# Weights in contiguous tiles, and both halves of the weight split on GpSimd, in a one-core hybrid layer

## The chip, the cores and the metric

The kernel runs on one core of one Trainium2 chip. A core has TensorE (PE, matrix products into PSUM), VectorE (DVE), ScalarE (ACT), GpSimd (POOL) and SyncE (SP, which here issues the DMAs), and 16 DMA engines between HBM and the on-chip buffer. The metric is the device time of one launch in microseconds (us), the median of three runs; lower is better.

## The reference

One layer of a diffusion backbone for 256 context tokens and 2048 latent tokens of width 1024, all in float32:

```python
mod_ctx = (jnp.einsum('d,dn->n', jax.nn.silu(c_ctx), w_ada[l]) + b_ada[l])[None]
mod_lat = jnp.einsum('bd,dn->bn', jax.nn.silu(c), w_ada[l]) + b_ada[l]
...
shift, scale, gate = jnp.split(mod, 3, axis=-1)
h = rmsnorm(x, g_pre) * (1.0 + scale[:, None]) + shift[:, None]
proj = jnp.einsum('btd,dn->btn', h, w_in)
...                       # NA, DeltaNet and pooling branches on slices of proj
merged = (g_dn * jnp.einsum('btw,wd->btd', y_dn, w_br_dn)
          + g_na * jnp.einsum('btw,wd->btd', y_na, w_br_na)
          + g_pl * jnp.einsum('btw,wd->btd', y_pl, w_br_pl))
out = rmsnorm(jnp.einsum('btd,de->bte', merged, w_out), g_post)
return x + gate[:, None] * out, k_na, v_na, s_fin
```

`w_in` has 8208 columns: q, k, v of the DeltaNet branch (1536), its gate path z (512), 16 columns for beta and a, q, k, v and z of the neighbourhood attention (4 x 512), u and z of the pooling branch (2 x 512), and the three merge gates (3072). The DeltaNet branch runs a short convolution with a SiLU over its q, k, v and then a recurrence over chunks; the attention branch has windows of 8 x 16 on a grid of 32 x 64 and all context keys.

## The kernel before

**Tiles.** The tokens are five blocks: C (256 context tokens) and L0 to L3 (512 latent tokens each). h is kept transposed, eight tiles of 128 channels by the block's tokens. Products of float32 are made of three products of a reduced type: each operand is split into a high part (a cast to fp32r) and a low part (the remainder), and `mm3` adds high x high, high x low and low x high. `split` (L167 to 170) is the helper for this: a cast on ACT (L169), then a subtraction on an engine that the caller names (L170).

**Weights of the input projection.** A unit is 128 columns of `w_in`. `load_w` (L552) loads it in two DMAs of 256 KB, each four 128x128 tiles side by side, into `wraw` (three buffers). ACT casts the 128x512 into `whi`, GpSimd subtracts into `wlo`; both have five buffers (`WBUFS`), two for a unit. `proj` (L566) then runs 24 matrix products for a block into a PSUM buffer `mm` (two of these). In HBM a row of such a tile is four pieces of 512 B, 32,832 B apart.

**Stages.** At the start `ada_part` (L427) loads eight pieces of `w_ada` of 1 MB each for shift and scale (a row is eight pieces of 1 KB) and multiplies them by the two conditioning vectors; beside it x of C and L0 is normalised and transposed, and `make_h` (L506) makes h: ACT the high part `hL0h`, DVE the full value `hf` (also kept in buffers named `x`, L522), GpSimd or DVE the low part `hL0l` (L523). Then `qkv` (L613) goes over C, L0 and L1, and again over L2 and L3. For each unit of q, k, v of DeltaNet, ACT copies the PSUM to `xcL` (L630) or `xcC` (L589), and `conv_silu` (L572) does DVE, then a tanh on ACT (`cv_th`, L580), then DVE, and stores to `d_dn`. Then, for eight units of attention q and k, ACT copies to `nqk` (L656, L658). Between these the 32 pieces of the attention's value weights (128x256, 128 KB) are loaded into the same three `nqk` buffers and split into `wvh` and `wvl` (L642 to L647), and the values are computed. Then `rest` (L1106) runs over the other units of `w_in`, for C, L2 and L3 and then for L0 and L1: gate paths (`zc`, copied at L1123), merge gates (a tanh `th`, L1131) and pooling. The branches (DeltaNet, whose steps end in names like `v` L1041; attention, with `pr`, `oT`, `klo`) run beside the projections. `final` (L1473) loads `w_br` in 120 tiles of 256 KB (`br_r`, four pieces of 512 B a row), splits them and merges.

**Order.** PE runs in the order of the program text. There a planner decides: `mm` advances a clock `self.t` by an estimate, `use` (L96) books time on `v`, `s` or `g` (DVE, ACT, GpSimd), and `poll` (L71) takes up the side branches whenever their due time has come. ACT, DVE, GpSimd and SP are ordered by the framework's scheduler, except where `dma_here` or `keep_in_program_order` fixes an instruction. All DMAs are issued from SP.

Of the kernel before, what the change touches and what calls it, by code (L numbers as in the profile page):

```python
# [7 lines left out]
F32 = mybir.dt.float32  # L8
# [3 lines left out]
ALU = mybir.AluOpType  # L12
# [4 lines left out]
P = 128  # L17
D = 1024
KT = 8
# [6 lines left out]
C_QKV, C_DZ, C_BA = 0, 1536, 2048  # L26
C_NQ, C_NK, C_NV, C_NZ = 2064, 2576, 3088, 3600
# [11 lines left out]
NQ = 3  # L39
# [8 lines left out]
class Net:  # L48
# [378 lines left out]
    def ada_part(self, q):  # L427

        nc = self.nc
        ps = self.mmp.tile([P, 512], F32, name="mm")  # L430
        for s in range(2):
            t = self.ap.tile([P, KT, 256], F32, name="w_ada", bufs=3)
            self.dma_here(t, self.a["w_ada"].rearrange("(k p) n -> p k n", p=P)[:, :, s * D + q * 256:s * D + q * 256 + 256])
            for k in range(KT):
                for c in range(2):
                    self.mm(ps[64 * s + 32 * c:64 * s + 32 * c + 32, :P], self.ada_sc[:, k, :], t[:, k, c * P:(c + 1) * P], k == 0, k == KT - 1)
        r = self.wp.tile([P, 4, P], F32, name="wraw", bufs=3)[:, 0]
        nc.scalar.copy(r, ps[:, :P])
        tp = self.ax1()[:, :P]
        self.tr(tp, r, self.ident)  # L440
        part = lambda t: t.rearrange("p (s k) x -> p s k x", s=2)[:, :, 2 * q:2 * q + 2]
        nc.vector.tensor_tensor(part(self.mod), tp.rearrange("p (s k x) -> p s k x", s=2, k=2)[:, :, :, 0:2],
                                part(self.cc["b_ada"].rearrange("p (c o) -> p c o", o=1)).broadcast_to([P, 2, 2, 2]), ALU.add)
        k = slice(2 * q, 2 * q + 2)
        g = self.cc["g_pre"]
        nc.vector.scalar_tensor_tensor(self.A[:, k], self.mod[:, 8 + 2 * q:10 + 2 * q, :], 1.0,
                                       g[:, k].rearrange("p (k o) -> p k o", o=1).broadcast_to([P, 2, 2]), ALU.add, ALU.mult)

    def ada_gate(self):

        nc, a = self.nc, self.a
        ps = self.ax1()

        for k in range(KT):
            t = self.ap.tile([P, D], F32, name="w_ada", bufs=3)
            self.dma_here(t, a["w_ada"][k * P:(k + 1) * P, 2 * D:])
            yield self.t + 5
            for c in range(4):
                self.mm(ps[32 * c:32 * c + 32, :256], self.ada_sc[:, k, :], t[:, c * 256:(c + 1) * 256], k == 0, k == KT - 1)
        r, bg, gp = (self.ap.tile([P, 256], F32, name=f"ada_{x}", bufs=1) for x in "rbg")  # L460
        for c in range(4):
            q = slice(32 * c, 32 * c + 2)
            for t, v in ((bg, a["b_gate"]), (gp, a["g_post"])):
                self.dma(t[q], bass.AP(v.tensor, v.offset + c * 256, [[0, 2], [1, 256]]))
            nc.vector.tensor_tensor(r[q], ps[q, :256], bg[q], ALU.add)
            nc.vector.tensor_tensor(r[q], r[q], gp[q], ALU.mult)
            self.dma(self.d_gg[:, c * 256:(c + 1) * 256], r[q])
# [84 lines left out]
    def load_w(self, c0, dma=None):  # L552
        hi, lo = [], []
        for k in (0, 4):
            raw = self.wp.tile([P, 4, P], F32, name="wraw", bufs=3)
            (dma or self.dma)(raw, self.a["w_in"].rearrange("(k p) n -> p k n", p=P)[:, k:k + 4, c0:c0 + P])
            h = self.wp.tile([P, 4, P], F32R, name="whi", bufs=WBUFS)
            l = self.wp.tile([P, 4, P], F32R, name="wlo", bufs=WBUFS)
            self.split(raw, h, l, self.nc.gpsimd)
            self.use("s", 0.52)  # L560
            self.use("g", 1.23)
            hi += [h[:, i] for i in range(4)]
            lo += [l[:, i] for i in range(4)]
        return hi, lo
# [48 lines left out]
    def qkv(self, h, second, nxt, first=None):  # L613
        nc = self.nc
# [21 lines left out]
        wv = [[self.qp.tile([P, KT, 264], F32R, name=x, bufs=2) for x in ("wvh", "wvl")] for _ in range(2)]  # L636

        raw = self.qp.tile([P, KT, 16], F32, name="wba", bufs=1)
        self.dma(raw, self.a["w_in"].rearrange("(k p) n -> p k n", p=P)[:, :, C_BA:C_BA + 16])
        for c in range(2):  # L640
            self.split(raw[:, :, 8 * c:8 * c + 8], wv[c][0][:, :, 256:264], wv[c][1][:, :, 256:264], nc.vector)
        for ct in range(8):  # L642
            for k in (2 * ct % 8, 2 * ct % 8 + 1):
                c = ct // 4
                raw = self.qp.tile([P, 512], F32, name="nqk", bufs=NQ)
                self.dma(raw[:, :256], self.a["w_in"][k * P:(k + 1) * P, C_NV + c * 256:C_NV + c * 256 + 256])
                self.split(raw[:, :256], wv[c][0][:, k, :256], wv[c][1][:, k, :256], nc.gpsimd)  # L647
            isq = ct < 4
            w = self.load_w(C_NQ + ct * P)
            r = slice((ct % 4) * P, (ct % 4 + 1) * P)  # L650
            for b in h:
                n = BLK[b]
                ps = self.proj(w, h[b], n)
                e = self.qp.tile([P, 512], F32, name="nqk", bufs=NQ)
                if isq:
                    nc.scalar.activation(e[:, :n], ps[:, :n], AF.Copy, scale=0.125)  # L656
                else:
                    nc.scalar.copy(e[:, :n], ps[:, :n])  # L658
                if b == "C":
                    self.dma((self.d_nq if isq else self.d_nk)["C"][r, :], e[:, :n])  # L660
                    if not isq:
                        self.add(self.new_k(e, r))
                else:
                    o = int(b[1]) * 512 + (0 if isq else CTX)
                    self.dma((self.d_nq if isq else self.d_nk)["L"][r, o:o + 512], e)

        for b in sorted(h, key=lambda b: b == "C"):
            for j in range(0, BLK[b] // P, 2):
                for c in range(2):
                    e = self.qp.tile([P, 528], F32, name="ev", bufs=2)  # L670
                    t = (0 if b == "C" else 2 + 4 * int(b[1])) + j
                    for i in range(2):
                        ps = self.mmp.tile([P, 512], F32, name="mm")
                        s = slice((j + i) * P, (j + i + 1) * P)
# [798 lines left out]
    def final(self, b, ys, nxt):  # L1473
        nc, f = self.nc, self.fin
        v, s = nc.vector, nc.scalar
        n = BLK[b]
# [6 lines left out]
        for m in range(KT):  # L1483
            if m:
                next(self.wo, None)
            acc = None
            for bi in range(3):
                raw = f.tile([P, 4, P], F32, name="br_r", bufs=BR)
                self.dma(raw, self.a["w_br"][bi].rearrange("(k p) n -> p k n", p=P)[:, :, m * P:(m + 1) * P])
                wh = f.tile([P, 4, P], F32R, name="br_h", bufs=BH)  # L1490
                wl = f.tile([P, 4, P], F32R, name="br_l", bufs=BH)
                self.split(raw, wh, wl, v if b == "C" and bi else nc.gpsimd)
                gt = f.tile([P, 512], F32, name="gt", bufs=GT)
                self.dma(gt[:, :n], self.d_g[b][m, :, bi, :])
                ps = self.mmp.tile([P, 512], F32, name="mm")
                yh, yl = ys[bi]
                for k in range(4):
                    self.mm3(ps[:, :n], wh[:, k, :], wl[:, k, :], yh[:, k, :n], yl[:, k, :n], k == 0, k == 3)
                v.scalar_tensor_tensor(gt[:, :n], gt[:, :n], 1.0, ps[:, :n], ALU.add, ALU.mult)  # L1499
                if acc is None:  # L1500
                    acc = gt
                else:
                    v.tensor_tensor(acc[:, :n], acc[:, :n], gt[:, :n], ALU.add)  # L1503
            mh[m] = self.fw.tile([P, 512], F32R, name="mh", bufs=8)
            ml[m] = self.fw.tile([P, 512], F32R, name="ml", bufs=8)
            s.activation(mh[m][:, :n], acc[:, :n], AF.Copy, scale=0.25)
            v.scalar_tensor_tensor(ml[m][:, :n], acc[:, :n], 0.25, mh[m][:, :n].bitcast(F32), ALU.mult, ALU.subtract)
# [40 lines left out]
def lay_out(i):  # L1548

    import numpy as np  # L1550
    f = lambda x: np.ascontiguousarray(np.asarray(x))
    cols = lambda x, k: f(np.asarray(x).reshape(k, P).T)
    d = {}
# [4 lines left out]
    d["cache_k"] = f(i["cache_k_na"]).reshape(CTX, 512)  # L1558
    d["cache_v"] = f(i["cache_v_na"]).reshape(CTX, 512)
    d["state_dn"] = f(i["state_dn"]).reshape(2, 4, P, P)  # L1560
    d["w_ada"] = f(i["w_ada"]).reshape(D, 3 * D)
    ba = np.asarray(i["b_ada"]).reshape(3 * D)
    d["b_ada"] = cols(ba[:2 * D], 16)
    d["b_gate"] = f(ba[2 * D:])
    d["g_pre"] = cols(i["g_pre"], KT)
    d["g_post"] = f(i["g_post"]).reshape(D)
    d["w_in"] = f(i["w_in"]).reshape(D, -1)
    d["conv"] = f(np.asarray(i["conv_dn"]).reshape(3, 12, P).transpose(2, 1, 0))
    d["a_log"] = f(i["a_log_dn"]).reshape(8)
    d["dt_bias"] = f(i["dt_bias_dn"]).reshape(8)  # L1570
    d["g_norm"] = cols(i["g_norm_dn"], 1)
    d["pool_w"] = f(i["pool_w"]).reshape(4, P, P)
    d["pool_scale"] = cols(i["pool_scale"], 4)
    d["w_br"] = f(np.stack([np.asarray(i[n]).reshape(512, D) for n in ("w_br_dn", "w_br_na", "w_br_pl")]))
    d["w_out"] = f(i["w_out"]).reshape(D, D)

    nb = np.pad(np.asarray(i["na_bias"]).reshape(8, 15, 31), ((0, 0), (4, 3), (16, 16)))
    q, k = np.arange(16)[:, None], np.arange(32)[None, :]
# [4 lines left out]
    ct = (r // 16) % 3  # L1583
    qc = np.array((0, 16, 48))[ct] + r % 16
    s = np.clip(qc - 8, 0, 48)[:, None]
# [31 lines left out]
```

## Time and profile before

| quantity | value |
|---|---|
| median of 3 runs | 2995.29 us (2993.88 to 2996.5) |
| the profiled execution's own time | 2992.84 us |
| its span in the trace | 2991.1 us |
| mean granted clock of TensorE | 0.972 |
| PE, DVE, ACT, POOL busy | 94%, 49%, 36%, 32% |
| DMA traffic | 492.26 MB, mean 165 GB/s |

A row of the waits names the engine and its line that waited, what it waited for, the total in us, how often and the longest. A row of a timeline begins with the start in us and the duration; then come engine, line, operation, output<-input, shapes, and in brackets how long the engine had been idle and for what. A row that groups by line has the number of instructions, then busy us and the mean ns of one, then the idle time ahead of them with what ended it. A row of the windows has start:end and length, then for PE, PEld (weight loads of PE), DVE, ACT and POOL the busy us with the number of instructions, then the granted PE clock (1.00 is full), the mean busy share of the 16 DMA engines, and GB/s.

### The profile page before, as it was taken

The numbers are of one execution on the slowest core, as the hardware profiler recorded it, in microseconds if no ns is written. First come the engines' busy times: TensorE is split into PE (matmuls) and PEld (weight loads), VectorE is DVE, ScalarE is ACT, GpSimd is POOL, SyncE is SP. The second block draws the span as 40 slices with busy tenths as digits, with TensorE's granted clock in tenths as the row PEclk, the third lists the DMA queues.
The fourth block names the chain that finished last, engine by engine and source line by source line (L and its number), as shares of the span: only waits on it lengthen the run. The fifth ranks groups of instructions, "written<-read, shape, count | busy, mean of one in ns | idle before, by whom it ended". The sixth has DMA issues, their size and how long they took to land.

```text
span 2991.1 us, 49701 instructions
## 1 busy us (share of the span) xinstructions
PE 2809.6 (94%) x18254; PEld 2374.8 (79%) x18254; DVE 1462.6 (49%) x3128; ACT 1061.9 (36%) x2505; POOL 944.6 (32%) x1152
## 2 busy tenths in 40 slices
PE   6899998999889999999899898899999999999998
PEld 5788986788777888878678887678888877787787
DVE  5651044301376554555623565466666516456555
ACT  5332232222333332424323355345445423222222
POOL 3222241230233231323311034432222145555542
PEclk9999999999999999999999999999999999999999
DMA  8433346543555464545549895545555367666654
GB/s 268 116 87 104 104 142 194 154 127 87 159 159 172 109 191 121 175 125 165 132 115 302 277 296 182 143 136 147 149 147 140 94 201 239 198 203 200 203 177 143
DMA packets 496995, 492.26 MB, mean 165 GB/s; under 512 B 77256, under 2 KB 382704, under 8 KB 496752
## 3 DMA queue, kind: packets, MB, share of 16 engines
q1 hardware_dynamic: 496752, 489.09, 55.6%
q8 instruction: 144, 2.36, 0.3%
q14 instruction: 99, 0.81, 0.1%
HBM read 347.13 MB, written 155.60 MB: 168 GB/s over the span
## 4 chain that ended last, share of the span: by engine, by line
PE 38%; DMA 11%; DVE 4%; POOL 3%; ACT 3%; issue 2%; SPq 1%; POOLq 0%; ACTq 0%; DVEq 0%
PE mm L155 22%; PE ax L155 6%; PE sx L155 5%; PE sx L159 3%; DMA yz<-d_zL 2%; PE fo L155 2%; POOL yo L1468 1%; DMA d_of<-o 1%; DMA xo<-w_out 1%; DMA wraw<-w_in 1%; SPq L139 1%; DMA raw<-d_nkL 1%; DMA o<-d_of 1%; DVE yl L170 1%; DVE gt L1503 0%
## 5 line engine op out<-in xcount | busy, mean ns | idle before, releaser
L170 POOL TENSOR_TENSOR wlo<-wraw,whi 128x512 fp32r<-128x512 f32 x240 | 317.9, 1327 | 759.6 <-ACT whi L169 651.6
L155 PE MATMUL mm<-hL0h,whi 128*128 128x512 f32 x960 | 404.5, 421 | 33.9 <-ACT xcL L630 13.7
L155 PE MATMUL mm<-hL1h,whi 128*128 128x512 f32 x960 | 395.0, 411 | 13.8 <-ACT xcL L630 5.6
L155 PE MATMUL mm<-hL0l,whi 128*128 128x512 f32 x960 | 384.6, 401 | 1.0 <-POOL hL0l L170 1.0
L155 PE MATMUL mm<-hL0h,wlo 128*128 128x512 f32 x960 | 384.0, 400 | 0.0
L155 PE MATMUL mm<-hL1l,whi 128*128 128x512 f32 x960 | 379.8, 396 | 1.6 <-DVE hL1l L523 1.3
L155 PE MATMUL mm<-hL1h,wlo 128*128 128x512 f32 x960 | 379.4, 395 | 0.0
L155 PEld LDWEIGHTS mm<-hL0h,whi 128*128 128x128 f32 x960 | 186.7, 194 | 77.2 <-ACT xcL L630 15.2
L169 ACT CAST whi<-wraw 128x512 fp32r<-128x512 f32 x240 | 147.7, 620 | 234.4 <-PE mm L155 188.7
L155 PEld LDWEIGHTS mm<-hL1h,whi 128*128 128x128 f32 x960 | 183.1, 191 | 57.3 <-ACT xcL L630 6.4
L155 PEld LDWEIGHTS mm<-hL0h,wlo 128*128 128x128 f32 x960 | 185.6, 193 | 41.1
L155 PEld LDWEIGHTS mm<-hL1h,wlo 128*128 128x128 f32 x960 | 182.9, 191 | 39.5
L155 PEld LDWEIGHTS mm<-hL0l,whi 128*128 128x128 f32 x960 | 186.8, 195 | 33.3 <-POOL hL0l L170 1.5
L155 PEld LDWEIGHTS mm<-hL1l,whi 128*128 128x128 f32 x960 | 183.3, 191 | 35.5 <-DVE hL1l L523 1.8
L155 PE MATMUL mm<-yh,br_h 128*128 128x512 f32 (+1 forms) x480 | 179.3, 374 | 18.9 <-DVE gt L1499 18.1
L170 POOL TENSOR_TENSOR br_l<-br_r,br_h 128x512 fp32r<-128x512 f32 x104 | 147.9, 1429 | 147.1 <-ACT br_h L169 145.7
L155 PE MATMUL mm<-yh,br_l 128*128 128x512 f32 (+1 forms) x480 | 178.3, 371 | 0.0
L155 PE MATMUL mm<-yl,br_h 128*128 128x512 f32 (+1 forms) x480 | 178.0, 371 | 0.0
L1375 DVE CUSTOM_DVE_ANT_0 pr<-sx,tab 128x736 f32<-128x736 f32 (+2 forms) x128 | 105.7, 864 | 86.0 <-PE sx L155 84.1
L1377 ACT ACTIVATE pr<-pr,mx 128x736 f32<-128x736 f32 (+2 forms) x128 | 109.6, 857 | 106.0 <-DVE mx L1375 105.7
L155 PE MATMUL mm<-hCh,whi 128*128 128x256 f32 x464 | 135.8, 293 | 11.9 <-ACT zc L1123 7.3
L155 PE MATMUL mm<-hCh,wlo 128*128 128x256 f32 x464 | 134.2, 289 | 0.0
(342 smaller groups left out, 5885.4 us busy)
## 6 DMA issues: line engine op xcount, KB each, us to landing
wraw<-w_in SPq DMA_DIRECT2D x240, 256.0 KB
br_r<-w_br SPq DMA_DIRECT2D x120, 256.0 KB
d_gL<-th SPq DMA_DIRECT2D x96, 256.0 KB
gt<-d_gL SPq DMA_DIRECT2D x96, 256.0 KB
skv<-d_kv SPq DMA_DIRECT2D x36, 512.0 KB
d_zL<-zc SPq DMA_DIRECT2D x48, 256.0 KB
yz<-d_zL SPq DMA_DIRECT2D x48, 256.0 KB
tab<-d_tab SPq DMA_DIRECT2D x48, 240.0 KB
```

The source lines that it names most:

```text
L139: return self.nc.sync.dma_start(out, in_)
L155: self.nc.tensor.matmul(out, lhsT=l, rhs=r, start=start, stop=stop)
L159: self.nc.tensor.transpose(out, in_, ident)
L169: self.nc.scalar.copy(hi, src)
L170: lo_eng.tensor_tensor(lo, src, hi.bitcast(F32), ALU.subtract)
L1375: nc.vector.tensor_tensor_reduce(out=pr[:, :nk], in0=ps[:, :nk], in1=tab[0][hh][:, :nk], scale=-1.0, scalar=3e38, op0=ALU.add, op1=ALU.min ...
L1377: nc.scalar.activation(pr[:, :nk], pr[:, :nk], AF.Exp, bias=mx, scale=-1.0, accum_out=sm)
L1468: self.nc.gpsimd.tensor_tensor(o[:, :n], o[:, :n], z[:, :n], ALU.mult)
```

## The change

Three things change. The host lays out four weight arrays so that each tile that the kernel loads is contiguous: `w_ada` for shift and scale (a row of a tile is now 8 KB), the units of `w_in` (`w_u`, rows of 2 KB), the value weights (`w_v`) and `w_br` (rows of 2 KB). The gate columns of `w_ada` become an array of their own with the same tiles as before. In `load_w` the cast to `whi` goes from ACT to GpSimd, where the subtraction is already; the planner books GpSimd for 2.4 us in two pieces in place of ACT for 0.52 and GpSimd for 1.23. The value weights are loaded in 16 pieces of 256 KB in place of 32 of 128 KB, each split in one step of 512 columns.

```diff
 def ada_part(self, q):
-            self.dma_here(t, self.a["w_ada"].rearrange("(k p) n -> p k n", p=P)[:, :, s * D + q * 256:s * D + q * 256 + 256])
+            self.dma_here(t.rearrange("p k n -> p (k n)"), self.a["w_ada"][s, q])
...
 def load_w(self, c0, dma=None):
-            (dma or self.dma)(raw, self.a["w_in"].rearrange("(k p) n -> p k n", p=P)[:, k:k + 4, c0:c0 + P])
+            u = (c0 - (C_NQ - C_BA if c0 > C_BA else 0)) // P
+            (dma or self.dma)(raw.rearrange("p k n -> p (k n)"), self.a["w_u"][u, k // 4])
...
-            self.split(raw, h, l, self.nc.gpsimd)
-            self.use("s", 0.52)
-            self.use("g", 1.23)
+            self.nc.gpsimd.tensor_copy(h, raw)
+            self.nc.gpsimd.tensor_tensor(l, raw, h.bitcast(F32), ALU.subtract)
+            self.use("g", 2.4, n=2)
...
 def qkv(self, h, second, nxt, first=None):
-            for k in (2 * ct % 8, 2 * ct % 8 + 1):
-                c = ct // 4
-                raw = self.qp.tile([P, 512], F32, name="nqk", bufs=NQ)
-                self.dma(raw[:, :256], self.a["w_in"][k * P:(k + 1) * P, C_NV + c * 256:C_NV + c * 256 + 256])
-                self.split(raw[:, :256], wv[c][0][:, k, :256], wv[c][1][:, k, :256], nc.gpsimd)
+            c, k = ct // 4, 2 * ct % 8
+            raw = self.qp.tile([P, 512], F32, name="nqk", bufs=NQ)
+            self.dma(raw, self.a["w_v"][c, :, k * 256:k * 256 + 512])
+            self.split(raw.rearrange("p (k n) -> p k n", k=2), wv[c][0][:, k:k + 2, :256], wv[c][1][:, k:k + 2, :256], nc.gpsimd)
...
 def final(...):
-                self.dma(raw, self.a["w_br"][bi].rearrange("(k p) n -> p k n", p=P)[:, :, m * P:(m + 1) * P])
+                self.dma(raw.rearrange("p k n -> p (k n)"), self.a["w_br"][bi, m])
...
 def lay_out(...):        # on the host
+    d["w_ada"] = f(w[:, :2 * D].reshape(KT, P, 2, 4, 256).transpose(2, 3, 1, 0, 4)).reshape(2, 4, P, KT * 256)
+    d["w_u"] = f(u.reshape(2, 4, P, -1, P).transpose(3, 0, 2, 1, 4)).reshape(-1, 2, P, 512)
+    d["w_v"] = f(w[:, C_NV:C_NZ].reshape(KT, P, 2, 256).transpose(2, 1, 0, 3)).reshape(2, P, KT * 256)
+    d["w_br"] = f(w.transpose(0, 3, 2, 1, 4)).reshape(3, KT, P, 512)
```

Lines from L554 on stand one further down in the changed kernel (the tanh of L580 is at L581, the copy of L630 at L631). GpSimd at the start of the kernel, before: `hL0l` is the low part of h of block L0, `wlo` that of the first weights, `rs` the scale of the next block's rows.

```order
L523 TENSOR_TENSOR hL0l<-hf,hL0h 128x512 x2
L170 TENSOR_TENSOR wlo<-wraw,whi 128x512 x2
L523 TENSOR_TENSOR hL0l<-x,hL0h 128x512
L170 TENSOR_TENSOR wlo<-wraw,whi 128x512 x2
L491 TENSOR_SCALAR rs<-ss 128x1
L523 TENSOR_TENSOR hL0l<-x,hL0h 128x512
L492 TENSOR_TENSOR rs<-rs,nhalf 128x1
```

And at the same place in the changed kernel:

```order
L523 TENSOR_TENSOR hL0l<-hf,hL0h 128x512 x2
L560 CAST whi<-wraw 128x512 x2
L561 TENSOR_TENSOR wlo<-wraw,whi 128x512 x2
L523 TENSOR_TENSOR hL0l<-x,hL0h 128x512
L560 CAST whi<-wraw 128x512 x2
L561 TENSOR_TENSOR wlo<-wraw,whi 128x512
L491 TENSOR_SCALAR rs<-ss 128x1
L561 TENSOR_TENSOR wlo<-wraw,whi 128x512
L523 TENSOR_TENSOR hL0l<-x,hL0h 128x512
```

Four casts come in, two ahead of the subtraction of the third `hL0l` and two ahead of that of the fourth.

ACT in the DeltaNet units of the second half (L2 and L3), before: `xcL` is the copy out of PSUM, `cv_th` the tanh of the convolution.

```order
L169 CAST whi<-wraw 128x512
L580 ACTIVATE cv_th<-cv_t 128x512
L169 CAST whi<-wraw 128x512
L630 COPY xcL<-mm 128x512 x2
L169 CAST whi<-wraw 128x512
L580 ACTIVATE cv_th<-cv_t 128x513
L169 CAST whi<-wraw 128x512
L630 COPY xcL<-mm 128x512
L580 ACTIVATE cv_th<-cv_t 128x512
```

The same engine and stage in the changed kernel:

```order
L631 COPY xcL<-mm 128x512
L581 ACTIVATE cv_th<-cv_t 128x513
L631 COPY xcL<-mm 128x512
L581 ACTIVATE cv_th<-cv_t 128x512
L631 COPY xcL<-mm 128x512
L581 ACTIVATE cv_th<-cv_t 128x513
L631 COPY xcL<-mm 128x512
```

The casts are gone, and copies and tanhs alternate; no copy has a cast between it and the tanh ahead of it.

## Rows read from the trace of the kernel before

**Rows 1.** The page, busy us (share) and instructions of each engine.

```profile
PE 2809.6 (94%) x18254; PEld 2374.8 (79%) x18254; DVE 1462.6 (49%) x3128; ACT 1061.9 (36%) x2505; POOL 944.6 (32%) x1152
```

**Rows 2.** Waits of PE over the whole span.

```profile
PE mm L155 <- ACT xcL L630: 19.9, 7, 6.4
PE mm L155 <- ACT th L1131: 19.5, 11, 4.0
...
PE ax L155 <- ACT v L1041: 11.5, 10, 4.3
PE mm L155 <- ACT zc L1123: 11.1, 3, 7.3
PE ax L159 <- DMA Q<-d_dnC: 8.6, 1, 8.6
...
PE mm L155 <- DMA w_ada<-w_ada: 5.6, 1, 5.6
...
PE mm L155 <- ACT nqk L656: 3.1, 3, 1.4
```

**Rows 3.** Timeline of ACT, 160 to 190 us.

```profile
163.77 0.62 ACT L169 CAST whi<-wraw 128x512 fp32r<-128x512 f32 x1 [2.10 <-PE mm L155]
...
177.57 0.62 ACT L169 CAST whi<-wraw 128x512 fp32r<-128x512 f32 x1 [2.10 <-PE mm L155]
```

**Rows 4.** Lines by form, GpSimd's subtractions and ACT's casts for the weights.

```profile
L170 POOL TENSOR_TENSOR wlo<-wraw,whi 128x512 fp32r<-128x512 f32 x240 | 317.9, 1327 | 759.6 <-ACT whi L169 651.6 <-PE ax L155 72.6 <-DVE rs L1387 10.2
L169 ACT CAST whi<-wraw 128x512 fp32r<-128x512 f32 x240 | 147.7, 620 | 234.4 <-PE mm L155 188.7 <-issue 24.8 <-DMA wraw<-w_in 17.3
```

**Rows 5.** Windows of the start, of projections and of attention.

```profile
4.00:9.00 5.00, 0.00 (x0) 0.00 (x0) 0.68 (x1) 2.30 (x4) 0.94 (x3) 1.00 0.99 359
14.00:30.00 16.00, 12.10 (x146) 10.23 (x145) 7.93 (x17) 8.91 (x17) 4.22 (x9) 0.79 0.92 295
30.00:42.00 12.00, 5.92 (x84) 5.33 (x85) 9.91 (x19) 7.44 (x14) 4.50 (x4) 0.84 0.98 292
150.00:225.00 75.00, 75.00 (x399) 64.91 (x398) 42.17 (x72) 23.36 (x45) 14.98 (x25) 1.00 0.34 89
1680.00:1720.00 40.00, 36.15 (x274) 34.03 (x273) 21.90 (x61) 14.82 (x52) 2.54 (x2) 1.00 0.89 295
```

**Rows 6.** Timeline of all engines, 40 to 44 us.

```profile
41.99 2.35 PE L155 MATMUL mm<-w_ada,ada_sc 128*32 128x128 f32 x20 [5.60 <-DMA w_ada<-w_ada]
...
43.23 1.27 POOL L523 TENSOR_TENSOR hL0l<-x,hL0h 128x512 fp32r<-128x512 f32 x1 [2.99 <-DVE x L522]
```

**Rows 7.** Timelines of ACT and PE, 468 to 472 us.

```profile
469.16 0.63 ACT L580 ACTIVATE cv_th<-cv_t 128x513 f32<-128x513 f32 x1 [7.92 <-DVE cv_t L578]
469.70 0.60 ACT L169 CAST whi<-wraw 128x512 fp32r<-128x512 f32 x1
470.21 0.58 ACT L630 COPY xcL<-mm 128x512 f32<-128x512 f32 x1
...
470.84 0.50 PE L155 MATMUL mm<-hL1h,whi 128*128 128x512 f32 x1 [3.60 <-ACT xcL L630]
```

**Rows 8.** Packets of the DMA engines, 150 to 225 us and 1680 to 1720 us.

```profile
DMA packets 13411, 6.66 MB, mean 89 GB/s; under 512 B 1152, under 2 KB 13407, under 8 KB 13407
...
DMA packets 5570, 11.80 MB, mean 295 GB/s; under 512 B 526, under 2 KB 1550, under 8 KB 5566
```

**Rows 9.** GpSimd's copies, least/median/longest duration in ns.

```profile
L680 POOL COPY BA<-ev x18: 196/196/197, 352.9 to 699.8; 128x16 f32<-128x16 f32 x18
...
L393 POOL COPY x<-x x3: 393/859/862, 420.5 to 429.5; 128x256 f32<-128x256 f32 x3
```

**Rows 10.** Timelines of DVE, GpSimd and PE, 2005 to 2013 us.

```profile
2009.86 2.13 DVE L1388 TENSOR_SCALAR pr<-pr,rs 128x608 f32<-128x608 f32 x1
...
2009.89 1.27 POOL L1225 TENSOR_TENSOR klo<-raw,khi 128x512 fp32r<-128x512 f32 x1
...
2012.24 0.88 PE L159 MATMUL sx<-ident,pr 128*128 128x128 f32 x6 [1.33 <-DVE oT L1430]
```

More of the change, by code (lines that the diff above doesn't have):

```diff
@@ L455, in ada_gate @@
             t = self.ap.tile([P, D], F32, name="w_ada", bufs=3)
-            self.dma_here(t, a["w_ada"][k * P:(k + 1) * P, 2 * D:])
+            self.dma_here(t, a["w_adag"][k * P:(k + 1) * P, :])
             yield self.t + 5
@@ L638, in qkv @@
         raw = self.qp.tile([P, KT, 16], F32, name="wba", bufs=1)
-        self.dma(raw, self.a["w_in"].rearrange("(k p) n -> p k n", p=P)[:, :, C_BA:C_BA + 16])
+        self.dma(raw.rearrange("p k n -> p (k n)"), self.a["w_ba"])
         for c in range(2):
@@ L1560, in lay_out @@
     d["state_dn"] = f(i["state_dn"]).reshape(2, 4, P, P)
-    d["w_ada"] = f(i["w_ada"]).reshape(D, 3 * D)
+    w = np.asarray(i["w_ada"]).reshape(D, 3 * D)
+    d["w_ada"] = f(w[:, :2 * D].reshape(KT, P, 2, 4, 256).transpose(2, 3, 1, 0, 4)).reshape(2, 4, P, KT * 256)
+    d["w_adag"] = f(w[:, 2 * D:])
     ba = np.asarray(i["b_ada"]).reshape(3 * D)
@@ L1566, in lay_out @@
     d["g_post"] = f(i["g_post"]).reshape(D)
-    d["w_in"] = f(i["w_in"]).reshape(D, -1)
+    w = np.asarray(i["w_in"]).reshape(D, -1)
+    u = np.concatenate([w[:, :C_BA], w[:, C_NQ:]], axis=1)
+    d["w_u"] = f(u.reshape(2, 4, P, -1, P).transpose(3, 0, 2, 1, 4)).reshape(-1, 2, P, 512)
+    d["w_ba"] = f(w[:, C_BA:C_NQ].reshape(KT, P, 16).transpose(1, 0, 2)).reshape(P, KT * 16)
+    d["w_v"] = f(w[:, C_NV:C_NZ].reshape(KT, P, 2, 256).transpose(2, 1, 0, 3)).reshape(2, P, KT * 256)
     d["conv"] = f(np.asarray(i["conv_dn"]).reshape(3, 12, P).transpose(2, 1, 0))
@@ L1573, in lay_out @@
     d["pool_scale"] = cols(i["pool_scale"], 4)
-    d["w_br"] = f(np.stack([np.asarray(i[n]).reshape(512, D) for n in ("w_br_dn", "w_br_na", "w_br_pl")]))
+    w = np.stack([np.asarray(i[n]).reshape(4, P, KT, P) for n in ("w_br_dn", "w_br_na", "w_br_pl")])
+    d["w_br"] = f(w.transpose(0, 3, 2, 1, 4)).reshape(3, KT, P, 512)
     d["w_out"] = f(i["w_out"]).reshape(D, D)
```

## The prediction

> **What bounds the kernel now.** I read the page's busy times first, then what TensorE waited for, then the stretches in which DMA is full, then the timeline at single waits. TensorE (PE) is busy for 2809.6 of 2991.1 us [rows 1]: nothing that another engine saves is worth more than a share of the 181 us that are left, and each wait in them has its own cause. The largest are for ACT's copies out of PSUM in the projections, 19.9, 19.5, 11.1 and 3.1 us, and one of 5.6 us for a modulation weight at the start [rows 2]. No row of that view waits for `whi` or `wlo`, the two parts of a weight that the change makes on GpSimd alone. Five buffers, two to a unit, are why: a cast starts when PE frees a buffer (2.10 us of waiting for PE at 163.77, and again at 177.57 [rows 3]), so a unit takes 13.8 us there, and what is cast is wanted about one and a half units later, some 20 us. Cast and subtraction take 2 us together [rows 4]. Making weights is slack, and the change pays only where something else stood behind it: in DMA at the start, and in ACT's queue.
>
> **The change part by part.** The sum is made against the profiled execution's 2992.84 us. That is 1.0 us under the lowest and 2.5 under the median of the runs shown (2995.29), so I add the sum to the median.
>
> *Start, wider packets.* Eight loads of 1 MB for the modulation get 8 KB a row in place of eight pieces of 1 KB, and the weight loads 2 KB in place of four pieces of 512 B. From 14 to 42 us the 16 engines are 0.92 and 0.98 busy and move 295 and 292 GB/s. From 4 to 9 us, with rows of 4 KB among the pieces of 1 KB, they move 359 at 0.99, which is 363 at full share [rows 5]. 16 us x 295 and 12 us x 292 are 8.22 MB. Their busy time was 26.5 us and falls to 22.6 at 363, by 3.9. PE waits 5.60 us for the last of these loads at 41.99 [rows 6], so all 3.9 show, until DVE and GpSimd are late with the parts of h before it (a subtraction at 43.23 [rows 6]). Against it, GpSimd's queue gets four casts between its subtractions of h there, as the order in the section on the change shows. I take -3.5; bounds -5.6 (the whole wait) and +1 (casts in the way).
>
> The Trainium skill, "DMA: Bandwidth & Descriptors", section Specifications, gives 512 B as the least transfer at line rate. By it pieces of 1 KB lose nothing and this term would be 0. The rows move 12% more in a busy second when larger rows are among them, so the term stays.
>
> *ACT loses 240 casts*, 147.7 us of busy time, and with them 188.7 us in which it waited for PE to free `whi` [rows 4]. Most of that was idle time anyway. It counts only where a cast stood between the operation that ACT had waited for and the copy that PE waited for. At 469.16 ACT starts a tanh after 7.92 us of waiting for DVE, then a cast, 0.51 us from start to start, then the copy, and PE goes on at 470.84, 3.60 us late [rows 7]; 0.51 of it is the cast's. In the new order the copies there follow the tanh directly. I looked in this way at each of PE's waits of 0.9 us or more between 90 and 2450 us that ACT ended: nine have casts in between, eleven in all, the one above among them. 11 x 0.51 is 5.6. I take -5.5. It would be -53.6 if all that PE waits for these copies went [rows 2], and 0 if the next late thing takes the place: the DVE operation before the tanh is not touched.
>
> *Value weights.* 32 loads of 128 KB become 16 of 256 KB and take one buffer of the three at a time where they took two. PE's three waits for the copies that share these buffers (`nqk`) are 3.1 us [rows 2]. I take -2; bounds -3.1 and +1 (one cast of 512 columns ahead of the copy in place of two of 256).
>
> *Lighter DMA after the start.* 240 x 262,144 B are 62.9 MB. Where nearly all packets are below 2 KB (13,407 of 13,411), 89 GB/s take 0.34 of the engines, 262 at full share; where 4,000 of 5,570 are 2 KB or more, 295 take 0.89, 331 [rows 5, 8]. That is 240 us against 190: 50 us of all engines, and the 31.5 MB of the last stage's projections give 25 more, together 2.5% of the span. It shows only where PE's wait ends in a DMA: 8.6 us for Q alone, and part of the 19.9 us for the copies behind the convolution [rows 2]. I take -3; bounds 0 and -10.
>
> *GpSimd gets 240 casts.* The trace has no cast there. A copy takes 0.196 us for 16 columns, and for 256 it takes 0.393 at least and 0.859 at the median of three [rows 9]: 0.82 ns a column, 0.60 us for 512, and 1.07 if I add the difference between those two. That is 145 to 257 us on an engine which is 32% busy [rows 1], with some 20 us of slack a weight: nothing for the weights. Its cost is in DVE's time. At 2009.86 a DVE operation takes 2.13 us and ends 0.83 us after a subtraction on GpSimd that began as it did, and PE goes on 1.33 us late [rows 10]. I take +3, between the nearest row, two more such hits, and none. Bounds: 0, and 1.33 in each of PE's 34 waits for ACT's copies and for `v` [rows 2], +45.
>
> The Trainium skill, "SBUF — State Buffer", section Who interferes with whom, says that DVE and GpSimd share a port pair which is locked for a whole instruction, and that a DVE operation with two inputs from there contends with any GpSimd instruction that reads. The rows at 2009.86 agree for a DVE operation with one tensor input. By this rule more casts mean more hits, which is the third rival.
>
> *Order.* The planner no longer books ACT for a weight and books GpSimd twice, so PE's side work stands some matmuls earlier or later: 0, within 8 either way.
>
> The sum: -3.5 - 5.5 - 2 - 3 + 3 = -11, and -1.5 for the clock, which is granted at 0.79 and 0.84 between 14 and 42 us, partly at 1.2 GHz, where PE waits [rows 5]. From 2995.3 that is **2983 us**, 0.4% less.
>
> **The rivals.** *Nothing to measure*, about 2994. Weights had 20 us of slack, DMA is half free after the start, and what ACT gains goes over into the next wait, on DVE. For it: the tanh before the copy at 470.21 had waited 7.92 us for DVE [rows 7], with or without a cast. Against it: the 5.6 us at the start are a plain wait for a load.
>
> *More than I count*, about 2962. In the projections ACT has little but copies left, the order makes them earlier, and half of the 53.6 us go: -27 for -5.5. For it: 188.7 us in which ACT's queue stood before a cast [rows 4]. Against it: while it stood there, it was PE's work that it waited for.
>
> *Slower*, about 3010. Casts on GpSimd lock DVE out on PE's path: cast, subtraction, cast, subtraction hold GpSimd for 3.8 us on end. If two thirds of the 34 waits grow by 1.33 us, that is 30 in place of 3, and the sum becomes +14.5. It decides from 16 of the 34, where 21 us bring the result 6 us above the old one. For it: the rows at 2009.86. Against it: GpSimd already works a third of the time, and PE's waits for DVE itself are short (none among the longest of [rows 2]).
>
> **How the numbers follow.** The forecast 0.51 (its own range 2975 to 2990), nothing 0.19, more 0.15, slower 0.15. Runs of this kernel tell 0.2%, 6 us, from no change: faster is below 2989.3, slower above 3001.3. Nearly all of 0.51 and the 0.15 are faster, 0.64; the same 0.20; slower 0.16. For 8 in 10 the range goes into both far cases: 2961 to 3003.
>
> **What would show it.** PE's wait for a modulation weight near 42 us under 2 us, and the first projection some 4 us earlier. PE's waits for the four copies under 48 us in place of 53.6. ACT's busy time down by 148 us and GpSimd's up by some 145, a cast at 0.6 us (at 1.1 the slower rival gains). All 16 engines' share of DMA time down by 2 points or more at the same bytes. I am wrong if PE waits for `whi` or `wlo` anywhere after 60 us, if its waits for DVE grow by over 10 us, or if the start is no shorter.

## The result, and the profile after

The changed kernel takes 2877.79 us (median of 4 runs, 2869.59 to 2883.16) against 2994.59 of the kernel before: a ratio of 0.9596, 95% interval 0.9574 to 0.9619. It is 117 us faster where 12 were forecast, and lies far below the range.

The page of the changed kernel, its first section, stands against [rows 1]. The same 18,254 matrix products take 36.9 us less of PE's time, and the span is 113.8 us shorter:

```profile
PE 2772.7 (96%) x18254; PEld 2351.3 (82%) x18254; DVE 1505.6 (52%) x3128; ACT 931.5 (32%) x2249; POOL 1104.9 (38%) x1376
```

The mean granted clock went from 0.972 to 0.984, and 2809.6 x 0.972 / 0.984 is 2775: the products are cheaper by the clock. The other 76.9 us are waiting. When I add all idle times of PE above 0.1 us in both traces, there are 97 of them with 173.5 us before and 66 with 96.7 after; those that ended in ACT fall from 86.2 to 26.6 us, in a DMA from 20.1 to 6.3, in DVE from 61.8 to 56.8. Waits of PE after, for [rows 2]:

```profile
PE mm L155 <- ACT zc L1123: 5.0, 1, 5.0
PE mm L155 <- ACT xcL L631: 4.7, 4, 2.8
PE ax L159 <- DMA Q<-d_dnC: 4.5, 1, 4.5
...
PE mm L155 <- ACT th L1131: 3.4, 3, 1.7
...
PE ax L155 <- ACT v L1041: 2.6, 3, 1.4
...
PE mm L155 <- DMA w_ada<-w_ada: 1.6, 1, 1.6
```

The four copies for which PE waited 53.6 us cost 13.1 now, with no row left for `nqk`. This looks like the rival in which ACT, rid of its casts, is early with its copies; the experiments say otherwise. The weight's two parts on GpSimd, against [rows 4]:

```profile
L561 POOL TENSOR_TENSOR wlo<-wraw,whi 128x512 fp32r<-128x512 f32 x240 | 324.3, 1352 | 14.5
L560 POOL CAST whi<-wraw 128x512 fp32r<-128x512 f32 x240 | 157.6, 657 | 660.9 <-PE mm L155 629.5 <-DMA wraw<-w_u 30.8
```

The cast takes 0.657 us there (0.60 was taken), and as before it waits for PE to free a buffer, 629.5 us in all: weights still have slack.

The DMA queue has the same bytes in fewer packets, and takes 53.2% of the span where it took 55.6:

```profile
q1 hardware_dynamic: 347248, 489.09, 53.2%
```

### The profile page after: what moved, and what is told of

It reads as the page before. It is cut to its first block, busy times and chain, and to the rows that moved or that the text cites. A ratio compares the mean times of both kernels' runs of the same rounds, so it can differ in the third digit from the quotient of the medians.

```text
span 2877.3 us, 49702 instructions
## 1 busy us (share of the span) xinstructions
PE 2772.7 (96%) x18254; PEld 2351.3 (82%) x18254; DVE 1505.6 (52%) x3128; ACT 931.5 (32%) x2249; POOL 1104.9 (38%) x1376
## 3 DMA queue, kind: packets, MB, share of 16 engines
q1 hardware_dynamic: 347248, 489.09, 53.2%
## 4 chain that ended last, share of the span: by engine, by line
PE 44%; DMA 6%; DVE 4%; POOL 3%; issue 2%; ACT 2%; SPq 0%; POOLq 0%; ACTq 0%; DVEq 0%
PE mm L155 26%; PE ax L155 7%; PE sx L155 6%; PE sx L159 3%; DMA yz<-d_zL 2%; PE fo L155 2%; POOL yo L1468 1%; DMA xo<-w_out 1%; DVE yl L170 1%; DMA o<-d_of 1%; PE ax L159 1%; DVE tm L892 0%; DVE Y L893 0%; DVE gt L1503 0%; DVE gt L1499 0%
## 5 line engine op out<-in xcount | busy, mean ns | idle before, releaser
L560 POOL CAST whi<-wraw 128x512 fp32r<-128x512 f32 x240 | 157.6, 657 | 660.9 <-PE mm L155 629.5
L155 PE MATMUL mm<-hL0h,whi 128*128 128x512 f32 x960 | 395.8, 412 | 10.9 <-ACT xcL L631 4.7
L155 PE MATMUL mm<-hL1h,whi 128*128 128x512 f32 x960 | 392.3, 409 | 5.0 <-ACT zc L1123 5.0
L155 PE MATMUL mm<-hL0l,whi 128*128 128x512 f32 x960 | 379.2, 395 | 6.5 <-POOL hL0l L170 6.5
L155 PE MATMUL mm<-hL1l,whi 128*128 128x512 f32 x960 | 376.8, 393 | 1.1 <-DVE hL1l L523 0.9
L561 POOL TENSOR_TENSOR wlo<-wraw,whi 128x512 fp32r<-128x512 f32 x240 | 324.3, 1352 | 14.5
```

The costliest lines, as they stand in the source:

```text
L155: self.nc.tensor.matmul(out, lhsT=l, rhs=r, start=start, stop=stop)
L560: self.nc.gpsimd.tensor_copy(h, raw)
L561: self.nc.gpsimd.tensor_tensor(l, raw, h.bitcast(F32), ALU.subtract)
```

## The experiments

Each time is a median, each ratio is to the kernel before, run beside it on the same chip, with its 95% interval. A difference between two experiments is taken from their ratios.

### Which part of the change

My first theory, A, was that the cast in ACT's queue had held back copies, and stores on SP behind full weight buffers. Its rivals: B, the layout; C, the planner's order. The booking is the time that the planner writes down for ACT and GpSimd, by which it places PE's side work. First the new layout with the cast and the booking of before:

```diff
 # the changed kernel, load_w
-            self.nc.gpsimd.tensor_copy(h, raw)
-            self.nc.gpsimd.tensor_tensor(l, raw, h.bitcast(F32), ALU.subtract)
-            self.use("g", 2.4, n=2)
+            self.split(raw, h, l, self.nc.gpsimd)
+            self.use("s", 0.52)
+            self.use("g", 1.23)
```

> All four arrays laid out in contiguous tiles and the value weights in 16 loads, but the cast stays on ACT and the planner books it as before. Theory A (the cast in ACT's queue held back copies out of PSUM, and through the weight buffers SP's queue and the stores behind it): a small part of the 117 us, about -10 to -25, with PE's waits for xcL, th and zc near those of before (together over 35 us). Theory B (smaller packets held up the transfers on which everything waits): most of it, -60 to -100, and the waits for xcL and th mostly gone. Theory C (the planner's other order on PE): near 0 to -25, as in A.

2872.85 us, 0.9604 (0.9588 to 0.9620). The layout alone has the whole gain, more than B had it at, and PE's waits for `xcL` and `th` are 2.5 and 4.5 us. A and C fall as its cause. Three kernels with the old layout: the cast and the booking moved; the booking alone; the cast alone.

```diff
 # the kernel before, load_w
-            self.split(raw, h, l, self.nc.gpsimd)      # not in the second kernel
+            self.nc.gpsimd.tensor_copy(h, raw)
+            self.nc.gpsimd.tensor_tensor(l, raw, h.bitcast(F32), ALU.subtract)
-            self.use("s", 0.52)                        # not in the third kernel
-            self.use("g", 1.23)
+            self.use("g", 2.4, n=2)
```

> Layout of before; cast on GpSimd with the new booking. A: -80 to -105, PE's waits for xcL, th, zc together under 20 us. B: -10 to -40. C: like A, so only with the next two kernels does this one tell A from C.

2972.35 us, 0.9935 (0.9919 to 0.9951).

> Nothing of the work is changed: the cast stays on ACT, the layout is that of before, only the planner books GpSimd for 2.4 us in place of ACT 0.52 and GpSimd 1.23, so PE's side work stands in the order that a cast on GpSimd would give it. A: within 15 us of before. B: 0. C: -40 or more.

2974.41 us, 0.9939 (0.9920 to 0.9957).

> Layout of before, cast on GpSimd, but the planner books as if it were on ACT, so PE's order is that of before. A: nearly all that the kernel with cast and new booking gains, within 20 us of it. B: -10 to -40. C: near 0.

2978.92 us, 0.9957 (0.9942 to 0.9972). On the old layout each is worth 12 to 19 us, and both together no more than one. No theory had the 17 us of the booking alone (A had up to 15, B 0, C 40 or more), and what in PE's new order brings them these runs do not show.

### Which loads

Only the units of `w_in` contiguous, and everything but these:

```diff
 # the kernel before, load_w
-            (dma or self.dma)(raw, self.a["w_in"].rearrange("(k p) n -> p k n", p=P)[:, k:k + 4, c0:c0 + P])
+            (dma or self.dma)(raw.rearrange("p k n -> p (k n)"), self.a["w_u"][u, k // 4])
 # the other kernel: the layout-only kernel with the removed line in place of the added one
```

> Of the layout only the 240 loads of the input projection's units are contiguous (rows of 2 KB); w_ada, the value weights and w_br as before, cast on ACT, booking as before. If these loads are what counts (their time from issue to landing is 5.63 us at the median before and 2.95 with the whole layout): -80 to -105. If the other arrays carry it: -40 or less.

2874.8 us, 0.9587 (0.9565 to 0.9610).

> w_ada, value weights and w_br contiguous, the units from the weights as they were; cast on ACT, booking as before. If the units are what counts: -10 to -25, most of it in the first 60 us and where the value weights are loaded. If the others carry it: -60 or more.

3002.6 us, 1.0000 (0.9983 to 1.0017), where 10 to 25 us less were expected. All of the gain is in the 240 loads of units; `w_ada`, the value weights and `w_br` in contiguous tiles bring nothing. With only the units laid out anew, and ACT still casting, PE's waits for ACT's copies are nearly gone. From its waits, where `zc` and `nqk` do not appear any more:

```profile
PE mm L155 <- ACT th L1132: 4.3, 3, 2.8
...
PE ax L155 <- ACT v L1042: 4.2, 6, 1.5
...
PE mm L155 <- ACT xcL L631: 2.5, 2, 1.5
```

So what PE waited for was ACT, and what made ACT late was a transfer. One such chain, before, from the timelines of SP and DVE ahead of the copy in [rows 7]:

```profile
457.92 0.56 SPq L139 DMA_DIRECT2D d_dnB<-cv_t  x1
...
466.99 0.49 DVE L576 TENSOR_SCALAR cv_t<-xcL,conv 128x513 f32<-128x513 f32 x1 [11.30 <-DMA d_dnB<-cv_t]
```

The store of a convolution's result is issued at 457.92, between loads of weights. Its buffer is free 9 us later, DVE has stood still for 11.30, the tanh at 469.16 comes after DVE, the copy after the tanh, and PE waits 3.60 us. DVE's total for this store, before and then after:

```profile
DVE cv_t L576 <- DMA d_dnB<-cv_t: 55.4, 12, 11.3
```

```profile
DVE cv_t L577 <- DMA d_dnB<-cv_t: 23.3, 9, 4.9
```

The other waits are of this kind. Followed back through the trace of the kernel before, from each wait to what ended it and through work without a break, all 27 of PE's waits for these copies (54.7 us with the few of L658) lead to a transfer: 19.9 us to stores of convolutions, 18.9 to stores of `Dm` to `d_at`, whose buffers DVE needs again, and the rest to six other loads and stores. In many of them the transfer had landed before PE began to wait, and the work behind it was what was late.

### How a slow load reaches PE

From the trace's completion events I take the time from a load's issue to the last of its completions: 5.63 us at the median of 240 unit loads before, 2.95 in the layout-only kernel; 3.53 for `w_br`'s loads before, 3.37 contiguous. Three theories for how this costs time: L, the weight itself is late; Q, what stands behind it in SP's queue is; E, it keeps the DMA engines from others. A kernel with late weights and fast loads, and two that issue the loads from GpSimd:

```diff
 # units contiguous, load_w
-            raw = self.wp.tile([P, 4, P], F32, name="wraw", bufs=3)
+            raw = self.wp.tile([P, 4, P], F32, name="wraw", bufs=2)
...
 # the kernel before, and units contiguous
-            (dma or self.dma)(raw,
+            (dma or self.nc.gpsimd.dma_start)(raw,
```

> Contiguous units as in the kernel with only these, but two buffers for loaded weights in place of three, so that loads are issued later and weights are there later, with nothing else on DMA made slower. Theory L (it is the late weight that costs: it holds up ACT's cast, and through full buffers SP's queue): the gain shrinks to -70 or less. Theory E (slow loads hold up the other transfers on the same DMA engines): -100 or more, within 20 us of contiguous units with three buffers.

2880.42 us, 0.9606 (0.9575 to 0.9636). The weights are later: at the median a weight is cast 9.2 us after it landed, where it was 19.2 with three buffers and 17.0 in the kernel before. It costs next to nothing, so L falls.

> Weights in the old rows, but their loads are issued from GpSimd's queue in place of SP's; all else as before. Theory Q (the slow loads hold up what stands behind them in SP's queue of issues): -60 or more without any change of layout. Theory E (they hold up the engines, whichever queue issues them): within 25 us of before.

3009.15 us, 1.0035 (1.0017 to 1.0052). Q falls, if issuing from GpSimd costs little; the control has that price.

> Control for the one before: contiguous units issued from GpSimd's queue. All theories: like contiguous units issued from SP, -100 to -125; what is lost against these is the price of issuing from GpSimd, and to be added to the gain of the old rows issued there.

2888.87 us, 0.9634 (0.9600 to 0.9668). The price is 14 us against contiguous units issued from SP, so the old rows, 10 us slower there, gain some 4 us by the other queue. Stores to `d_dnB` do land sooner there, 3.70 us after their issue at the median in place of 6.05, but PE's waits for `th` grow from 19.5 us [rows 2] to 30.5. A smaller part for the queue is not excluded, since issuing a load keeps GpSimd busy for 784 ns with the old rows and 580 with contiguous units. E is left. Issued from GpSimd, the loads have a row of their own in the profile (queue: packets, MB, share of 16 engines; then the load with its median time to landing). Old rows:

```profile
q0 software_dynamic: 18880, 61.88, 16.0%
...
wraw<-w_in POOLq DMA_DIRECT2D x236, 256.0 KB, 5.8
```

Contiguous units:

```profile
q0 software_dynamic: 18880, 61.88, 7.3%
...
wraw<-w_u POOLq DMA_DIRECT2D x236, 256.0 KB, 3.2
```

As many packets and bytes take 16.0% of 3009.4 us in place of 7.3% of 2882.1, 481 us of every engine against 210. Issued from GpSimd, a load in the old rows occupies the engines more than twice as long. Issued from SP the difference is smaller. The whole queue before, then with only the units contiguous:

```profile
q1 hardware_dynamic: 496752, 489.09, 55.6%
```

```profile
q1 hardware_dynamic: 404592, 489.09, 54.3%
```

Of 2991.1 us and 2865.3 this is 1663 us of every engine against 1556. The rest of the traffic goes through the same engines. From issue to landing the 1,741 other DMAs take 4.27 us on average before and 3.72 with the units contiguous, though their own packets are no slower before (those of 4 KB take 186 ns, and 192 with the units contiguous). So what they lose lies before their packets run, as E has it; packets of their own that take longer do not show.

### Why the old rows are slow

The old distance is that of two rows of `w_in`, 32,832 B. It lies between the pieces of neighbouring partitions; the four pieces of one partition, which the section on the kernel before also puts 32,832 B apart, are 128 rows apart (`(k p) n -> p k n`), 4,202,496 B. Padding a row changes both, and the runs below do not part them. S: 512 B are too small a piece. M: the pieces begin off a multiple of 512 B. One copy of the units with rows 33,280 B apart, still in pieces of 512 B; the same with every piece 64 B further on; and rows of 2 KB at multiples of 2,112 B:

```diff
 # the kernel before: load_w from a copy u of the units' columns, host
-            (dma or self.dma)(raw, self.a["w_in"].rearrange("(k p) n -> p k n", p=P)[:, k:k + 4, c0:c0 + P])
+            (dma or self.dma)(raw, self.a["w_p"].rearrange("(k p) n -> p k n", p=P)[:, k:k + 4, u * P:u * P + P])
+    d["w_p"] = f(np.pad(u, ((0, 0), (0, 128))))
...
 # second kernel: columns 16 + u * P on, and
+    d["w_p"] = f(np.pad(u, ((0, 0), (16, 112))))
...
 # third kernel
+            (dma or self.dma)(raw.rearrange("p k n -> p (k n)"), self.a["w_u"][u, k // 4, :, 0:512])
+    d["w_u"] = f(np.pad(d["w_u"], ((0, 0), (0, 0), (0, 0), (0, 16))))
```

> As before, but the units come from a copy of the weights whose rows are 33,280 B apart in place of 32,832: still four pieces of 512 B a row and 512 packets a load, now all beginning at multiples of 512 B. Theory S (many small pieces make the load slow): no change, within 10 us, and a median of 5 us or more from issue to landing. Theory M (the pieces begin at odd multiples of 64 B, and that makes each slow): most of the gain of contiguous units, -60 or more, and landing near the 3.5 us that w_br's pieces of 512 B, which begin at multiples of 512 B, already take.

2884.18 us, 0.9617 (0.9599 to 0.9634), landing 3.16 us: S falls.

> The same padded copy as in the kernel with aligned pieces (rows 33,280 B apart, four pieces of 512 B), but every piece begins 64 B behind a multiple of 512 B. Theory M (a piece that begins off a multiple of 512 B is slow): the time of before, within 25 us, and 5 us or more from issue to landing. Rival (it was the distance of 32,832 B between rows, not where a piece begins): the gain stays, -100 or more.

2878.51 us, 0.9592 (0.9558 to 0.9626), landing 3.24 us: M falls, and the distance of rows is left.

> Units in rows of 2 KB, one packet each, but the rows are 2,112 B apart, so that they begin at multiples of 64 B and hardly ever of 512 B. S: like contiguous units, -80 or more. M: a part of it, -20 to -60, since each row still begins off the line but there are a quarter as many.

2873.33 us, 0.9583 (0.9569 to 0.9598): also against M, which had 20 to 60 us here. Two theories are on the distance: D, that rows near 32 KiB apart are slow, and V, that the drift of 64 B from row to row is. The same copy with other distances, by the columns of padding (0, 1040 and 32), and the kernel before with padding and no other edit:

```diff
+    d["w_p"] = f(np.pad(u, ((0, 0), (0, 1040))))
...
-    d["w_in"] = f(i["w_in"]).reshape(D, -1)
+    d["w_in"] = f(np.pad(np.asarray(i["w_in"]).reshape(D, -1), ((0, 0), (0, 112))))
```

> Four pieces of 512 B a row, all beginning at multiples of 512 B, rows exactly 32,768 B apart (the copy without padding). Theory D (rows that lie near 32 KiB apart collide in memory, since 32,768 and 32,832 are nearly the same, while 33,280 moves each row on by 512 B): slow as before or slower, 0 to +60. Theory V (the drift of 64 B from row to row is what is slow): fast, -100 or more.

2880.96 us, 0.9606 (0.9582 to 0.9630): fast, against D.

> Rows 36,928 B apart: as before each row begins 64 B further behind a multiple of 512 B than the last, but the distance is 36 KiB and 64 B. D: between, -30 to -120, by how far 36 KiB spreads the rows. V: no gain, within 25 us of before.

2876.85 us, 0.9591 (0.9566 to 0.9616): fast, against V.

> The kernel before with nothing changed but 112 columns of zeros behind the weights of the input projection, so that their rows are 33,280 B apart. D and V both: -100 to -125, the whole gain.

2881.44 us, 0.9606 (0.9577 to 0.9636): 112 columns of zeros are worth what the whole change is. Both theories in the form I gave them had fallen; last, the old distance in another array:

```diff
+    d["w_p"] = f(np.pad(u, ((0, 0), (0, 16))))
```

> The units come from a copy of the weights of their own, 8208 columns wide, so that its rows are 32,832 B apart exactly as in the kernel before, and it is another array at another place in memory. Theory D (the distance of 32,832 B is what is slow): no gain, within 25 us of before, 5 us or more from issue to landing. Theory P (that one array lay badly in memory): -100 or more, landing near 3.2 us.

3045.64 us, 1.0163 (1.0143 to 1.0184), landing 6.24 us: slow again in another array, so it is the distance and not the one array's place that takes the gain away. But it is also 48 us slower than the kernel before, where at most 25 were expected. Something beside the distance adds to it, the place of the array or the columns at which the pieces begin, and no run tells which.

> The same copy with rows 32,896 B apart (32 KiB and 128 B, where before had 32 KiB and 64 B). D, if a small step beyond 32 KiB is what collides: slow, 0 to -50. D, if it is 32,832 alone, or P: -100 or more.

2883.01 us, 0.9618 (0.9592 to 0.9643). Of five distances near one another (32,768, 32,832, 32,896, 33,280 and 36,928 B) only 32,832 is slow. The pages of two kernels that differ in the padding of the copy alone, first rows 32,896 B apart, then 32,832:

```profile
DMA packets 496995, 492.26 MB, mean 171 GB/s; under 512 B 77256, under 2 KB 382704, under 8 KB 496752
...
q1 hardware_dynamic: 496752, 489.09, 55.0%
```

```profile
DMA packets 496995, 492.26 MB, mean 162 GB/s; under 512 B 77256, under 2 KB 382704, under 8 KB 496752
...
q1 hardware_dynamic: 496752, 489.09, 61.8%
```

The packets are the same in number and bytes; they take 55.0% of 2883.7 us, 1586, and 61.8% of 3046.5, 1883. By the trace a packet of 512 B, of the units and of others, takes 29.4 and 49.6 ns on average. The kernel before lies between them, with 36.0 ns and 1663 us. And with the distance the old waits of PE come back, larger than in [rows 2]:

```profile
PE mm L155 <- ACT xcL L631: 27.3, 9, 5.0
PE mm L155 <- ACT th L1132: 22.8, 10, 5.2
PE mm L155 <- ACT zc L1124: 18.2, 4, 9.5
```

### What the cast is worth

The layout with the cast on ACT and the booking of the changed kernel:

```diff
 # the changed kernel, load_w
-            self.nc.gpsimd.tensor_copy(h, raw)
-            self.nc.gpsimd.tensor_tensor(l, raw, h.bitcast(F32), ALU.subtract)
+            self.split(raw, h, l, self.nc.gpsimd)
```

> The whole layout with the cast on ACT, but the planner books as in the changed kernel. If casts on GpSimd and the booking are worth nothing on the new layout: within 10 us of the changed kernel and of the layout alone (2868 to 2885). If the booking is worth here what it was on the old rows (17 us): about 2858.

2862.85 us, 0.9548 (0.9523 to 0.9572): faster than both kernels, 17 us below the layout alone, where only the booking differs, and 14 below the changed kernel, where only the cast does (the intervals just do not overlap). The cast on GpSimd costs about what the booking gains. Its page:

```profile
PE 2763.6 (97%) x18254; PEld 2345.8 (82%) x18254; DVE 1463.8 (51%) x3128; ACT 1060.1 (37%) x2489; POOL 942.9 (33%) x1136
```

DVE does the same 3,128 instructions in 41.8 us less than in the changed kernel. The changed kernel's timeline has the reason, the same operation beside a subtraction on GpSimd and alone:

```profile
427.56 1.61 DVE L577 TENSOR_SCALAR cv_t<-xcL,conv 128x512 f32<-128x512 f32 x1 [4.94 <-DMA d_dnB<-cv_t]
...
441.93 0.49 DVE L577 TENSOR_SCALAR cv_t<-xcL,conv 128x512 f32<-128x512 f32 x1 [0.71 <-DMA d_dnB<-cv_t]
```

```profile
427.60 1.28 POOL L561 TENSOR_TENSOR wlo<-wraw,whi 128x512 fp32r<-128x512 f32 x1
```

DVE's row ends 0.3 us after GpSimd's. By lines, in the changed kernel the 24 of 512 columns take 641 ns on average:

```profile
L577 DVE TENSOR_SCALAR cv_t<-xcL,conv 128x512 f32<-128x512 f32 x24 | 15.4, 641 | 20.7 <-DMA d_dnB<-cv_t 19.0 <-DMA d_dnA<-cv_t 0.7 <-ACT xcL L631 0.4
```

In the changed kernel's trace 18 of the 24 run while GpSimd does nothing, 485 ns each, and six beside work on GpSimd, 1,109 each. With the cast on ACT the 24 take 523:

```profile
L576 DVE TENSOR_SCALAR cv_t<-xcL,conv 128x512 f32<-128x512 f32 x24 | 12.5, 523 | 5.0 <-DMA d_dnB<-cv_t 2.9 <-DMA d_dnA<-cv_t 1.0
```

PE's waits that end in DVE are 56.8 us in the changed kernel and 48.3 with the cast on ACT.

## Why the prediction was wrong, step by step

- **Lighter DMA after the start** is the step that failed. It was -3, with -10 as its end; it is nearly all of the 117 us. The engine time that it worked out was not the worst of it: 75 us less of all engines were estimated, and 132 were measured (55.6% of 2991.1 us, then 53.2% of 2877.3). Two things were wrong in it. I let it count only where PE's wait ends in a DMA. The view of waits names the last release; the 53.6 us for `xcL`, `th`, `zc` and `nqk` began in transfers, up to three steps further back, and the clock rose as they went. [Rows 7] had it in sight: the tanh waited 7.92 us for DVE, and I asked what stood between tanh and copy, not what DVE had waited for. And I put the difference of 262 and 331 GB/s down to the size of packets; with pieces of 512 B at another distance all of the gain is there.
- **The start.** Forecast -3.5; the first projection begins 4.7 us earlier and PE's wait there is 1.6 us in place of 5.6. But the main cause was not the wider rows of `w_ada`: with these and the old units the wait is still 5.0 us, and with contiguous units alone it is 4.2 us in two parts and the projection begins 3.5 us earlier. What was slow there were above all the weight loads beside `w_ada`. The sum had a slip: from 26.5 to 22.6 us is 17% more in a busy second, not 12. The rule that I set aside, the Trainium skill's "DMA: Bandwidth & Descriptors", section Specifications, by which pieces of 1 KB lose nothing, agrees with these runs as far as the kernel's time shows it (1.0000 with `w_ada`, the value weights and `w_br` in wider rows).
- **ACT loses 240 casts**: -5.5 forecast. On the old layout the cast alone brought 12 us, net of what GpSimd loses by it, and on the new layout it costs 14. The nine waits with casts in between went with the transfers, with the casts still on ACT.
- **GpSimd gets 240 casts**: the mechanism was right, DVE beside GpSimd, and the size too small: +3 was taken, and 14 us net of what ACT gains were measured, beside 41.8 us more of DVE's time. PE's waits for DVE were not short, as the prediction had it against the slower rival; these two rows of the kernel before are third and fourth of the view of [rows 2], and the second has the longest single wait of all:

```profile
PE mm L155 <- DVE gt L1499: 18.1, 11, 4.3
PE ax L159 <- DVE x L493: 13.6, 6, 9.1
```

- **Order**: 0 forecast, within 8; the booking alone brings 17 us on either layout.
- **Value weights**: -2 forecast; no run has them alone, but with `w_ada` and `w_br` they bring nothing.
- **The clock**: -1.5 forecast; 36.9 us of PE's busy time went with the waits. I counted each wait at its own length only.
- **The signs.** The wait near 42 us, the first projection, the copies under 48 us and the 2 points of DMA share (55.6% to 53.2%) came as named, and ACT and GpSimd moved the way that was named (-130 and +160 us); none of the three signs of being wrong came, PE's one wait for `wlo` being 0.2 us at 50 us. So the signs fitted a prediction whose main step was wrong: each was a bound on one side, and none told the casts from the transfers. That the kernel is faster, as forecast, is luck as far as the sum goes: all but a few us came from a term that it had at -3. The rival with more gain had the copies' waits go, but by ACT's casts, and -34 for it is also far from -117.

## What to carry to other kernels

Before the order of engines is touched, compare the loads of the same size and packet size by their time from issue to landing, or by bytes over engine time where they have a queue of their own. Where one array is slower than others, as `w_in` was here (5.63 us against 3.53 for `w_br`), try another distance of its rows by some padding; here one line on the host is worth the whole change. A wait for an engine is to be followed until it ends in something that has no wait of its own: the engine named last may be three steps from the cause.

## What the runs showed of the hardware

Rows 32,832 B apart make a load of 512 pieces of 512 B land in 5.6 to 6.2 us at the median, where rows 64 B nearer or further apart land in 3.2 to 3.3. Not every load at that distance is slow: the value weights, 128 pieces of 1 KB a load, keep it where only the units are contiguous, and land in 2.88 us (5.14 before). The Trainium skill, "DMA: Bandwidth & Descriptors", section Latency and other measured facts, tells of slow row pitches at large powers of two, from 512 KiB to 8 MiB, and names channels of memory that coincide as an inference. Here the power of two itself, 32,768 B, is fast, with 4 MiB between the four pieces of a partition, and a pitch 64 B above it slow, so for pieces of 512 B that rule does not tell which pitch to avoid. Why 32,832 is slow no run here shows.
